# One Griffin/S5 hybrid layer on a list scheduler: landing allowance, slot choice and the order of six pieces

## The chip, the cores and the metric

One core of one Trainium2 chip. The metric is the device time of one execution in microseconds, the median of the runs. Engines are named as in the profile: PE (TensorE, matmuls), PEld (its weight loads), DVE (VectorE), ACT (ScalarE), POOL (GpSimd), SP (SyncE, which only issues transfers).

## The reference, cut to what matters

All is float32, 1024 tokens by 1024 channels, one layer:

```python
mod = silu(c) @ mod_w + mod_b                  # 9 x 1024: shift, scale, gate for three norms
u = rms_norm(x, norm1_g) * (1 + sc1) + sh1
x = x + 0.5 * g1 * ((silu(u @ Wa) * (u @ Wb)) @ ffn1_w_down)        # 2816 wide
u = rms_norm(x, norm2_g) * (1 + sc2) + sh2
xa, ga, xb, mg_a, mg_b = split(u @ w_in + b_in)
ya = rg_lru(causal_conv(xa)) * gelu(ga)                             # linear scan over the tokens
yb = gelu(s5_ssm(xb)); yb = yb * sigmoid(yb @ glu_w + glu_b)        # complex scan
m = sigmoid(mg_a) * (ya @ proj_a) + sigmoid(mg_b) * (yb @ proj_b)
x = x + g2 * (m @ w_out)
u = rms_norm(x, norm3_g) * (1 + sc3) + sh3
x = x + 0.5 * g3 * swiglu(u)                                        # ffn2
out = rms_norm(x, final_g)
```

## The kernel before

Activations lie channel-first, in tiles of 128 channels by 512 tokens (two halves h). A float32 operand is split into `hi` (rounded, on ACT) and `lo` (the rest, on DVE), and a product is three matmuls: hi·hi, hi·lo, lo·hi. Most large products are done for two output blocks at once by a seven-product scheme (`pair`): seven products of 12 matmuls each (9 or fewer in the down-projections) instead of eight. They go through four PSUM banks a, b, c, d in the order 1 (a), 6 (b), 2 (onto a), 7 (onto b), 5 (c), 4 (d), 3 (onto c). After most products ACT or DVE evicts the bank (`tmp_in<-ps_in`). `pair_weights` makes the seven weight sums: it loads b, a and a second copy of half of b, S1, into a tile `re`; POOL adds to them by accumulating transfers (`plus`, shown as `wr_in<-wr_in`), and ACT and DVE split the results into `wh` and `wl`.

Nothing is issued in the order written. Every call is recorded, and `Plan.order` lays the calls out by a list schedule: on each engine the ready call with the smallest number goes first (loads of weights count as 200 calls earlier). A call that needs a new tile starts only where its pool has a free slot. Costs come from small formulas. A transfer of 256 KB from SP is taken to land 1300 + 60 + 728 + 900 ns after its issue, and an accumulating one 1000 + 1300 + 60 + 1456 + 900 ns; the last 900 is the allowance. The free slots of a pool are a list: freed slots are appended, and `pop()` takes the last one. The engines then run their queues strictly in that order, each call waiting on semaphores for what it reads or overwrites, so a wait holds all that is queued behind it. The pools: `act` 65 slots of 512 columns, `tmp` 6, `wr` 4, `wh` and `wl` 8 each, `re` 2, `mw` 1, `ps` 8 PSUM banks.

Side work runs as generators that `spread` steps on by a rate at each `tick`: the constants of the S5 part, the columns of `mod` (a 512 KB load and a DVE product with a reduction, in tile `mw`), the S5 units and the recurrence. `finish_jobs` runs out what is left.

Stages in the trace, by time: norm 1 and the first products to 90 us, ffn1 up (with the S5 constants) to about 550, ffn1 down to 716, the mixer's input projections to 1160 (`run`: first xb, then ga and mga by pairs, then xa and mgb alternating by `IN_ORDER`), `glu` to 1185, `proj_b` to 1237, `proj_a` to 1318, `w_out` to 1410, ffn2 to the end.

Of the kernel before, what the change touches and what calls it, by code (L numbers as in the profile page):

```python
# [35 lines left out]
OUT_POOL = ((), (0, 1, 2, 3, 4, 5, 6, 7), (1, 4, 7))  # L36
LED2 = 2
S5_RATE, LRU_RATE = 0.7, 1.0
IN_ORDER = [(k, n) for n in range(8) for k in ("xa", "mgb")]

SETUP_RATE, MOD_RATE, GAIN_RATE = 1.0, 0.15, 0.1

TAGS = {
    "act": (65, 512), "tmp": (6, 512), "sd": (1, 512), "wr": (4, 1024), "wh": (8, 512), "wl": (8, 512),
# [23 lines left out]
class Plan:  # L68
# [12 lines left out]
    }  # L81
    FLEXIBLE = ("vector", "scalar", "gpsimd")

    SUM_ISSUE = 1000.0

    EXTRA = {"vector": 0.0, "scalar": 0.0, "gpsimd": 600.0}
# [162 lines left out]
    def order(self):  # L249
# [51 lines left out]
        while done < n_ops:  # L301
            for e in self.ENGINES:
                if busy[e]:
                    continue
                held, item = [], None
                while ready[e] and len(held) < 64:
                    other = heappop(ready[e])
                    n = other[1]
                    if needs[n] and not fits(n):
                        held.append(other)  # L310
                        continue
                    if item is None:
                        item = other
                        if e != "scalar" or not self.switches(n, table):
                            break
                        continue

                    if other[0] > item[0] + SAME_TABLE:
                        held.append(other)
                        break  # L320
                    if not self.switches(n, table):
                        held.append(item)
                        item = other
                        break
                    held.append(other)
                for other in held:
                    heappush(ready[e], other)
                other, late = None, []
                while e in self.FLEXIBLE and ready["either"] and len(late) < 64:
                    one = heappop(ready["either"])  # L330
                    if item is not None and item < one:
                        late.append(one)
                        break
                    if e in self.other[one[1]] and (not needs[one[1]] or fits(one[1])):
                        if soonest(one) == e:
                            other = one
                            break
                    late.append(one)
                for one in late:
                    heappush(ready["either"], one)  # L340
                if other is not None:
                    if item is not None:
                        heappush(ready[e], item)
                    item = other
                    chosen[item[1]] = e
                    engine[item[1]] = e
                if item is None:
                    continue
                n = item[1]
                for t in needs[n]:  # L350
                    g = self.tag[t]
                    self.home[t] = g, free[g].pop()
                    queue[g].pop(bisect_left(queue[g], n))
                calls = self.calls(n)
                order.append(n)
                busy[e] = True
                if calls[0][1] == "dma_start":
                    size = 1
                    for s in calls[0][2][0].shape:
                        size *= s  # L360
                    if e == "gpsimd":
                        end = now + self.SUM_ISSUE
                        dma_free = max(dma_free, end + 1300) + 60 + size * 8 / 360
                        seen = dma_free + 900
                    else:
                        dma_free = max(dma_free, now + 1300) + 60 + size * 4 / 360
                        end, seen = now + 60, dma_free + 900
                else:
                    end = now
                    for c in calls:  # L370
                        ns, t = self.cost(c, table)
                        if e == "scalar":
                            table = t
                        if self.shares_port(c):
                            end = port_free = max(end, port_free) + ns
                        else:
                            end += ns
                    until[e] = end
                    seen = end + self.LATENCY[e][1]
                heappush(events, (end, len(order), e, n, 0))  # L380
                if calls[0][1] != "dma_start":
                    heappush(events, (end + self.LATENCY[e][0], len(order), e, n, 1))
                heappush(events, (seen, len(order), None, n, 2))
# [50 lines left out]
class Layer:  # L434
# [130 lines left out]
    def pair_weights(self, srcs):  # L565

        nc = self.nc
        n = srcs[0].shape[1] // 2
        with nc.ahead(WEIGHTS_AHEAD):
            a, b = self.new("wr"), self.new("wr")  # L570
            s1 = self.new("re")[:, :n]
            nc.sync.dma_start(b[:, : 2 * n], srcs[1])
            nc.sync.dma_start(a[:, : 2 * n], srcs[0])
            nc.sync.dma_start(s1, srcs[1][:, :n])
            a1, a2, b1, b2 = a[:, :n], a[:, n : 2 * n], b[:, :n], b[:, n : 2 * n]
            nc.scalar.activation(b1, b1, AF.Copy, scale=-1.0)
            nc.plus(b1, srcs[0][:, :n])
            nc.plus(s1, srcs[1][:, n : 2 * n])
            w = {1: self.split_weight(a1)}
            nc.scalar.activation(a1, b2, AF.Copy, scale=-1.0)  # L580
            nc.plus(a1, b1)
            w[2] = self.split_weight(a2)
            nc.plus(a2, a1)
            w[6] = self.split_weight(a1)
            w[7] = self.split_weight(b1)
            w[5] = self.split_weight(s1)
            w[4] = self.split_weight(b2)
            w[3] = self.split_weight(a2)
            return {k: [v] for k, v in w.items()}
# [137 lines left out]
        nc.vector.reciprocal(r, root)  # L727
        return r

    def modulate(self, x, r, l, d, pool=False):  # L730

        nc = self.nc
        nc.vector.scalar_tensor_tensor(
            x, x, self.gsc[:, l * 8 + d : l * 8 + d + 1], r, ALU.mult, ALU.mult
        )
        hi, lo = self.act(F32R), self.act(F32R)
        nc.scalar.activation(x, x, AF.Identity, bias=self.mod(3 * l, d))
        nc.rounded(hi, x)
        nc.two(ALU.subtract, lo, x, hi.bitcast(F32))
        return hi, lo  # L740
# [496 lines left out]
class Mixer:  # L1237
# [247 lines left out]
    def run(self):  # L1485
# [7 lines left out]
        for k in range(4):  # L1493
            for i, v in enumerate(u[1][k]):
                nc.scalar.dma_start(self.u_d[2 * k + i], v.bitcast(F32))
        L.spread(self.s5_units(), S5_RATE)
        for dst, i0, fn in ((self.ga_d, 8, AF.Gelu_apprx_tanh), (self.mga_d, 20, AF.Sigmoid)):
            for i in range(i0, i0 + 8, 2):
                c11, c12, c21, c22 = L.pair(
# [12 lines left out]
        for kind, n in IN_ORDER:  # L1512
# [5 lines left out]
            for h in range(2):  # L1518
                z = L.act()
                nc.scalar.activation(z, b[h], AF.Sigmoid, bias=L.col("b_in", 28 + n))  # L1520
                nc.sync.dma_start(self.mgb_d[n][:, h * H : (h + 1) * H], z)
        L.finish_jobs()
        yb = self.glu()
        for p in range(4):
            wp = L.weight(io["proj_b"][p])
            for e in range(2):
# [4 lines left out]
                    nc.vector.tensor_mul(r, r, b[h])  # L1531
                    nc.sync.dma_start(self.q_d[d][:, h * H : (h + 1) * H], r)
        ya = [[self.load(self.ya_d, n, h) for n in range(8)] for h in range(2)]
        ya = L.pair_operands(ya[0][:4], ya[0][4:], ya[1][:4], ya[1][4:], {})
        m = [[None] * 8, [None] * 8]
        for p, pair in enumerate(PROJ_A):
            c11, c12, c21, c22 = L.pair(L.pair_weights([io["proj_a"][d] for d in pair]), ya)
# [69 lines left out]
def hybrid_layer(ctx: ExitStack, tc: tile.TileContext, io):  # L1607
# [43 lines left out]
            nc.two(ALU.subtract, lo[:, o], raw, hi.bitcast(F32)[:, o])  # L1651

    first_weights(0)
    ps = L.bank()
    for d in range(ND):
        sq = L.act()
        nc.scalar.activation(sq, x[0][d], AF.Square)
        L.mm(ps, L.ones.bitcast(F32), sq, d == 0, d == ND - 1)
    u = [[], []]

    def step(h, k):
        u[h].append(L.modulate(x[h][k], rs[h], 0, k, pool=h == 1))
        for f in range(2):
            for j in range(2):
                L.products(
# [1 line left out]
                    k == 0, k == ND - 1,  # L1667
                )

    rs = [L.rstd_of(ps)]  # L1670
    L.modulation(1, 0, "wr")
    L.modulation(0, 0, "wr")
    for d in range(ND):
        load_x(1, d)
    step(0, 0)
    L.modulation(1, 1, "wr")
    L.modulation(0, 1, "wr")
    step(0, 1)
    st = [None]
    for d in range(ND):  # L1680
        L.square(st, x[1][d], d)
    rs.append(L.rstd(st))
    first_weights(2)
    step(1, 0)
    step(1, 1)
# [17 lines left out]
            L.modulation(*c)  # L1703
            yield

    later = modulations([(i, d) for i in (2, 4, 3, 5, 7, 6) for d in range(8)])

    def background():
        L.spread(s5_setup(L), SETUP_RATE)
        L.spread(later, MOD_RATE)  # L1710

    st = [[None], [None]]
    u2 = [[], []]
# [1 line left out]
    def on_x(d, h, x):  # L1715
# [5 lines left out]
                u2[h].append(L.modulate(x[h][e], r, 1, e))  # L1721

    L.up(w_up, u, x, 2, background)
    x = L.down(
        io["ffn1_w_down"], io["x"], None, 2, on_x, [(h, slice(0, H)) for h in range(2)], PARTS[0]
    )

    t = mixer(L, u2, x, x1_d)
    pieces = [(0, slice(0, H))] + [(1, slice(i * H // LAST, (i + 1) * H // LAST)) for i in range(LAST)]
    st3 = [[None] for _ in pieces]  # L1730
# [123 lines left out]
```

## Time and profile before

| | |
|---|---|
| median of 3 runs (lowest, highest) | 2077.71 us (2075.42, 2080.06) |
| the profiled execution, its span | 2080.47 us, 2078.7 us |
| PE, DVE, ACT, POOL busy | 96%, 75%, 50%, 16% of the span |
| mean granted clock of PE | 0.985 of full |
| HBM read, written | 280.90 MB, 92.27 MB |

Busy shares are means over stages with different limits. A busy PE is not PE at its peak: the ends of matmuls are modelled. The idle time before an instruction is put down to what released it, so "PE <-ACT tmp_in" is PE waiting until ACT has read a bank out.

### The profile page before, as it was taken

How to read it: one execution, taken by the hardware profiler on the slowest of the kernel's cores; microseconds unless marked ns; L12 is line 12 of the kernel's file. 1: busy time of each engine (PE TensorE's matmuls, PEld its weight loads, DVE VectorE, ACT ScalarE, POOL GpSimd, SP SyncE). 2: the span in 40 equal slices, each digit the busy share in tenths (PEclk: the TensorE clock that was granted, in tenths of full speed). 3: DMA queues.
4: the chain of work that ended last, by engine and by line, in shares of the span. 5: the costliest groups of instructions: out<-in, count | busy, mean ns of one | idle time of the engine just before them, and what ended most of it. 6: DMA issues, size and time to landing. Idle time of an engine off the chain costs nothing. (4 is left out here: it accounts for less than half of the span.)

```text
span 2078.7 us, 27418 instructions
## 1 busy us (share of the span) xinstructions
PE 1998.8 (96%) x8852; PEld 1632.3 (79%) x8852; DVE 1565.4 (75%) x3072; ACT 1036.2 (50%) x1774; POOL 322.9 (16%) x409
## 2 busy tenths in 40 slices
PE   5999999999999999999999999999999999999997
PEld 3787777887888878778888787777888888877786
DVE  8997877789969777768886886989644444498757
ACT  5633333435433574454878942446433333366643
POOL 0122111211011011100000001100111111124442
PEclk8999999999999999999999999999999999999998
DMA  8667777889857457787544858872765666589993
GB/s 275 178 168 204 196 201 204 218 221 287 279 150 217 153 153 217 204 250 263 173 158 132 282 175 252 267 250 72 193 170 139 151 158 157 131 215 235 212 230 123
DMA packets 198704, 411.18 MB, mean 198 GB/s; under 512 B 22176, under 2 KB 48416, under 8 KB 198560
## 3 DMA queue, kind: packets, MB, share of 16 engines
q1 hardware_dynamic: 132160, 296.54, 42.7%
q0 software_dynamic: 49536, 84.96, 24.3%
q10 hardware_dynamic: 16864, 27.93, 3.6%
q8 instruction: 69, 1.13, 0.2%
q14 instruction: 75, 0.61, 0.1%
HBM read 280.90 MB, written 92.27 MB: 180 GB/s over the span
## 5 line engine op out<-in xcount | busy, mean ns | idle before, releaser
L429 PE MATMUL ps_in<-act_in,wh_in 128*128 128x512 f32 (+1 forms) x5592 | 1691.5, 391 | 47.5 <-ACT tmp_in L429 14.5
L429 PEld LDWEIGHTS ps_in<-act_in,wh_in 128*128 128x128 f32 x5592 | 1048.8, 189 | 285.4 <-ACT tmp_in L429 21.0
L429 PE MATMUL ps_in<-act_in,wl_in 128*128 128x512 f32 (+1 forms) x2796 | 1049.8, 389 | 1.0 <-DVE wl_in L429 1.0
L429 PEld LDWEIGHTS ps_in<-act_in,wl_in 128*128 128x128 f32 x2796 | 529.3, 189 | 111.1 <-DVE wl_in L429 2.1
L429 ACT ACTIVATE wh_in<-wr_in 128x512 fp32r<-128x512 f32 (+2 forms) x544 | 321.1, 599 | 524.5 <-PE ps_in L429 363.3
L429 DVE TENSOR_TENSOR wl_in<-wr_in,wh_in 128x512 fp32r<-128x512 f32 (+2 forms) x544 | 350.9, 652 | 194.2 <-ACT wh_in L429 189.7
L429 DVE TENSOR_TENSOR act_in<-act_in,act_in 128x512 fp32r<-128x512 f32 (+3 forms) x589 | 375.9, 677 | 41.1 <-ACT act_in L429 34.4
L429 DVE TENSOR_TENSOR tmp_in<-ps_in,tmp_in 128x512 f32<-128x512 f32 x296 | 203.3, 687 | 143.6 <-PE ps_in L429 133.1
L429 ACT ACTIVATE act_in<-act_in 128x512 fp32r<-128x512 f32 (+3 forms) x413 | 238.2, 614 | 144.2 <-DVE act_in L429 107.0
L429 POOL DMA_DIRECT2D wr_in<-wr_in x148 | 135.3, 914 | 556.9 <-DMA wr_in<-wr_in 205.3
L429 ACT ACTIVATE wr_in<-wr_in 128x512 f32<-128x512 f32 (+1 forms) x148 | 87.7, 598 | 86.7 <-DMA wr_in<-in_ffn_w_up 48.6
L429 ACT ACTIVATE tmp_in<-ps_in 128x512 f32<-128x512 f32 x130 | 76.2, 588 | 42.6 <-PE ps_in L429 32.6
L429 DVE TENSOR_TENSOR tmp_in<-tmp_in,ps_in 128x512 f32<-128x512 f32 x82 | 56.0, 683 | 43.4 <-PE ps_in L429 42.8
L429 ACT ACTIVATE wh_in<-re_in 128x512 fp32r<-128x512 f32 (+1 forms) x74 | 44.4, 601 | 69.3 <-PE ps_in L429 69.1
L429 DVE SCALAR_TENSOR_TENSOR mw_in<-mw_in,cact 128x1024 f32<-128x1024 f32 x56 | 68.3, 1221 | 13.8 <-DMA mw_in<-in_mod_w 13.2
L429 POOL DMA_DIRECT2D re_in<-in_ffn_w_up x40 | 34.9, 880 | 246.3 <-DVE wl_in L429 120.6
L429 DVE TENSOR_TENSOR tmp_in<-tmp_in,tmp_in 128x512 f32<-128x512 f32 (+1 forms) x96 | 65.6, 686 | 3.8 <-DMA mga_d<-tmp_in 1.9
L429 ACT ACT_TABLE_LOAD x47 | 60.3, 1283 | 12.8 <-PE ps_in L429 9.9
L429 POOL DMA_DIRECT2D wr_in<-in_ffn_w_up x40 | 35.5, 887 | 182.8 <-ACT wr_in L429 147.1
L429 PE MATMUL ps_in<-act_in,act_in 128*128 128x256 f32 (+1 forms) x336 | 56.9, 317 | 4.4 <-DMA act_in<-sty_d 1.8
L429 DVE SCALAR_TENSOR_TENSOR act_in<-ps_in,mods,act_in 128x512 f32<-128x512 f32 (+1 forms) x68 | 46.1, 684 | 19.6 <-PE ps_in L429 19.4
L429 PEld LDWEIGHTS ps_in<-act_in,act_in 128*128 128x128 f32 x336 | 48.4, 190 | 13.4 <-ACT act_in L429 2.9
(109 smaller groups left out, 997.8 us busy)
## 6 DMA issues: line engine op xcount, KB each, us to landing
wr_in<-in_ffn_w_up SPq DMA_DIRECT2D x84, 512.0 KB, 4.4
mw_in<-in_mod_w SPq DMA_DIRECT2D x56, 512.0 KB, 4.3
wr_in<-wr_in POOLq DMA_DIRECT2D x108, 256.0 KB, 4.5
g_d<-tmp_in SPq DMA_DIRECT2D x88, 256.0 KB, 4.7
act_in<-g_d SPq DMA_DIRECT2D x88, 256.0 KB, 5.8
wr_in<-in_ffn_w_down SPq DMA_DIRECT2D x48, 384.0 KB, 5.0
wr_in<-in_w_in SPq DMA_DIRECT2D x36, 512.0 KB, 4.4
x_d<-tmp_in POOLq DMA_DIRECT2D x48, 256.0 KB, 6.8
```

Of the source, the lines that this page charges most:

```text
L429: getattr(getattr(self.nc, engine), method)(*map(self.place, args), **{k: self.place(v) for k, v in kwargs.items()})
```

## The change

- `LANDING`: the allowance for a landing in the plan is 1800 ns in place of 900.
- Slots: `free[g].pop(0)` takes the slot that has been free longest, in every pool.
- `modulate`: x/rms is a DVE product of two tensors, and scale and shift are together one ACT instruction (before: DVE did x·scale/rms, ACT the shift). For the first norm a new `norm(h)` multiplies all eight tiles ahead of the first products, and the sum of squares of the second half goes through float32 matmuls with ones, as that of the first half did (before: seven DVE additions, a split, two matmuls).
- `pair_weights`: S1 is an ACT copy of the loaded half of b, not a second load.
- `IN_ORDER`: the xa blocks come earlier; `glu` stands inside the loop, after mgb 6 and before mgb 7 (before: after all).
- `proj_a`'s operands are made product by product (`pair_operands_by_product`) instead of tile by tile.
- The columns of `mod`: 24 in ffn1 up at rate 0.18 and run out there, the other 24 in the mixer at 0.2 (before: all 48 from ffn1 up on at 0.15).

```diff
+    LANDING = 1800
-                    self.home[t] = g, free[g].pop()
+                    self.home[t] = g, free[g].pop(0)
-                        seen = dma_free + 900
+                        seen = dma_free + self.LANDING
...
-                        end, seen = now + 60, dma_free + 900
+                        end, seen = now + 60, dma_free + self.LANDING
...
-            nc.sync.dma_start(s1, srcs[1][:, :n])
             a1, a2, b1, b2 = a[:, :n], a[:, n : 2 * n], b[:, :n], b[:, n : 2 * n]
+            nc.scalar.activation(s1, b1, AF.Copy)
             nc.scalar.activation(b1, b1, AF.Copy, scale=-1.0)
...
-        nc.vector.scalar_tensor_tensor(
-            x, x, self.gsc[:, l * 8 + d : l * 8 + d + 1], r, ALU.mult, ALU.mult
-        )
-        nc.scalar.activation(x, x, AF.Identity, bias=self.mod(3 * l, d))
+        if r is not None:
+            nc.two(ALU.mult, x, x, r)
+        nc.scalar.activation(
+            x, x, AF.Identity, bias=self.mod(3 * l, d),
+            scale=self.gsc[:, l * 8 + d : l * 8 + d + 1],
+        )
...
+            if n == GLU_AFTER:
+                for _ in s5:
+                    pass
+                yb = self.glu()
         L.finish_jobs()
-        yb = self.glu()
...
-        ya = L.pair_operands(ya[0][:4], ya[0][4:], ya[1][:4], ya[1][4:], {})
+        ya = L.pair_operands_by_product(ya[0][:4], ya[0][4:], ya[1][:4], ya[1][4:])
...
+    def norm(h):
+        ps = L.bank()
+        for d in range(ND):
+            sq = L.act()
+            nc.scalar.activation(sq, x[h][d], AF.Square)
+            L.mm(ps, L.ones.bitcast(F32), sq, d == 0, d == ND - 1)
+        r = L.rstd_of(ps)
+        for d in range(ND):
+            nc.two(ALU.mult, x[h][d], x[h][d], r)
```

The order on DVE, in the second pair of `proj_a`. In the rows before, wl_2614 is the lo part of a sum that POOL adds (wh_2613 is split from it); `tmp<-ps` are evictions.

```order
L429 TENSOR_TENSOR act_2594_in<-act_2594_in,ps_2587_in 128x512
L429 TENSOR_TENSOR wl_2614_in<-wr_2606_in,wh_2613_in 128x512
L429 TENSOR_TENSOR wl_2616_in<-wr_2607_in,wh_2615_in 128x512
L429 TENSOR_TENSOR act_2594_in<-act_2594_in,act_2595_in 128x512
L429 TENSOR_TENSOR tmp_2591_in<-ps_2588_in,tmp_2591_in 128x512
```

The same place now, where the sum's lo part is wl_2604.

```order
L437 TENSOR_TENSOR act_2584_in<-act_2584_in,ps_2577_in 128x512
L437 TENSOR_TENSOR wl_2606_in<-wr_2597_in,wh_2605_in 128x512
L437 TENSOR_TENSOR act_2584_in<-act_2584_in,act_2585_in 128x512
L437 TENSOR_TENSOR tmp_2581_in<-ps_2578_in,tmp_2581_in 128x512
L437 TENSOR_TENSOR wl_2604_in<-wr_2596_in,wh_2603_in 128x512
```

The eviction of the pair's second bank stood behind the split of the sum and now stands ahead of it.

The order on PE where `glu` ends; its weights are wl_2382 before and wl_2362 now, those of `proj_b` wh_2402 and wh_2393. Before:

```order
L429 MATMUL ps_2381_in<-act_2353_in,wl_2380_in 128x512
L429 MATMUL ps_2382_in<-act_2355_in,wl_2380_in 128x512
L429 MATMUL ps_2406_in<-act_2385_in,wh_2402_in 128x512
L429 MATMUL ps_2406_in<-act_2386_in,wh_2402_in 128x512
L429 MATMUL ps_2407_in<-act_2393_in,wh_2402_in 128x512
```

Now:

```order
L437 MATMUL ps_2363_in<-act_2335_in,wl_2362_in 128x512
L437 MATMUL ps_2364_in<-act_2337_in,wl_2362_in 128x512
L437 MATMUL ps_2388_in<-act_1402_in,wh_2384_in 128x512
L437 MATMUL ps_2388_in<-act_1403_in,wh_2384_in 128x512
L437 MATMUL ps_2389_in<-act_1892_in,wh_2384_in 128x512
...
L437 MATMUL ps_2388_in<-act_1416_in,wl_2387_in 128x512
L437 MATMUL ps_2389_in<-act_1460_in,wl_2387_in 128x512
L437 MATMUL ps_2397_in<-act_2367_in,wh_2393_in 128x512
```

The 48 matmuls of the last input block (mgb 7, into ps_2388 and ps_2389) now stand between the last matmul of `glu` and the first of `proj_b`; before, these two followed each other.

The order on ACT, where the weight sums of the second pair of `proj_a` are begun; `act<-act` are the operands of all pairs, `wh` the splits of the first pair. Before:

```order
L429 ACTIVATE wh_2547_in<-wr_2535_in 128x512
L429 ACTIVATE act_2509_in<-act_2502_in 128x512
L429 ACTIVATE act_2511_in<-act_2463_in 128x512
L429 ACTIVATE wr_2607_in<-wr_2607_in 128x512
L429 ACTIVATE act_2513_in<-act_2501_in 128x512
```

Now:

```order
L437 ACTIVATE act_2496_in<-act_2454_in 128x512
L437 ACTIVATE re_2598_in<-wr_2597_in 128x512
L437 ACTIVATE wh_2539_in<-wr_2524_in 128x512
L437 ACTIVATE wr_2597_in<-wr_2597_in 128x512
L437 ACTIVATE act_2498_in<-act_2455_in 128x512
```

One ACT instruction more, the copy into `re`, stands ahead of the negation of the loaded half; so it is in all 74 pairs.

## Rows read from the trace of the kernel before

**Rows 1.** The page's first part: busy us, share of span, instructions by engine.

```profile
PE 1998.8 (96%) x8852; PEld 1632.3 (79%) x8852; DVE 1565.4 (75%) x3072; ACT 1036.2 (50%) x1774; POOL 322.9 (16%) x409
```

**Rows 2.** Stretches: length, busy PE, PEld, DVE, ACT, POOL, granted clock, DMA share, GB/s.

```profile
150.00:500.00 350.00, 340.87 (x1525) 276.63 (x1525) 276.97 (x656) 139.13 (x247) 69.42 (x96) 1.00 0.77 211
...
740.00:900.00 160.00, 148.87 (x669) 121.66 (x668) 114.34 (x192) 84.92 (x135) 23.17 (x32) 0.97 0.77 213
...
1160.00:1200.00 40.00, 35.78 (x143) 28.10 (x142) 34.09 (x57) 33.57 (x56) 0.86 (x1) 0.91 0.85 299
1200.00:1310.00 110.00, 106.19 (x460) 87.07 (x460) 80.50 (x137) 41.44 (x73) 13.01 (x15) 0.98 0.77 230
1310.00:1420.00 110.00, 101.83 (x422) 81.00 (x421) 97.24 (x160) 54.78 (x91) 7.82 (x9) 0.95 0.73 227
1420.00:1830.00 410.00, 409.86 (x1809) 339.12 (x1808) 222.38 (x341) 166.65 (x287) 70.21 (x81) 1.00 0.60 149
```

**Rows 3.** What PE waited for: total us, times, longest us.

```profile
PE ps_in L429 <- ACT tmp_in L429: 20.0, 15, 3.8
...
PE ps_in L429 <- DVE tmp_in L429: 9.6, 12, 2.6
```

**Rows 4.** Timeline in ffn1 up: start, us, engine, instruction, idle before and its releaser.

```profile
297.90 1.15 ACT L429 ACTIVATE wh_in<-wr_in 128x512 fp32r<-128x512 f32 x2 [7.33 <-DMA wr_in<-wr_in]
...
299.58 0.73 PE L429 MATMUL ps_in<-act_in,wh_in 128*128 128x512 f32 x2 [0.81 <-ACT tmp_in L429]
```

**Rows 5.** Timeline in the second pair of proj_a.

```profile
1268.20 1.15 ACT L429 ACTIVATE wh_in<-wr_in 128x512 fp32r<-128x512 f32 x2 [8.08 <-DMA wr_in<-wr_in]
...
1270.68 0.68 DVE L429 TENSOR_TENSOR tmp_in<-ps_in,tmp_in 128x512 f32<-128x512 f32 x1
...
1271.42 0.72 PE L429 MATMUL ps_in<-act_in,wh_in 128*128 128x512 f32 x2 [2.63 <-DVE tmp_in L429]
```

**Rows 6.** Timeline where the mixer's first projections end.

```profile
759.89 4.32 ACTq L429 DMA_DIRECT2D u_d<-act_in  x5
...
768.55 1.22 PE L429 MATMUL ps_in<-act_in,wh_in 128*128 128x512 f32 x2 [3.82 <-ACT tmp_in L429]
```

**Rows 7.** Timeline from glu to proj_b.

```profile
1185.68 0.73 PE L429 MATMUL ps_in<-act_in,wh_in 128*128 128x512 f32 x2 [1.64 <-ACT tmp_in L429]
1187.28 0.80 PE L429 MATMUL ps_in<-act_in,wh_in 128*128 128x512 f32 x1 [0.86 <-ACT act_in L429]
1189.32 0.79 PE L429 MATMUL ps_in<-act_in,wh_in 128*128 128x512 f32 x1 [1.25 <-DVE act_in L429]
...
1187.54 9.12 DVE L429 TENSOR_TENSOR act_in<-act_in,act_in 128x256 fp32r<-128x256 f32 x16
```

**Rows 8.** Timeline in the mixer's input projections.

```profile
864.41 0.60 ACT L429 ACTIVATE tmp_in<-ps_in 128x512 f32<-128x512 f32 x1 [3.79 <-DMA ga_d<-tmp_in]
...
865.06 0.73 PE L429 MATMUL ps_in<-act_in,wh_in 128*128 128x512 f32 x2 [2.08 <-ACT tmp_in L429]
...
889.81 1.45 PE L429 MATMUL ps_in<-act_in,act_in 128*128 128x256 f32 x10 [1.77 <-DMA act_in<-sty_d]
```

**Rows 9.** Transfers: kind, count, KB each, median us from issue to landing.

```profile
wr_in<-wr_in POOLq DMA_DIRECT2D x108, 256.0 KB, 4.5
...
ga_d<-tmp_in SPq DMA_DIRECT2D x16, 256.0 KB, 5.4
```

**Rows 10.** Groups of instructions: busy us, mean ns of one, idle before.

```profile
L429 PE MATMUL ps_in<-act_in,ones 128*128 128x512 f32 x16 | 9.8, 782 | 7.7 <-DVE sd_in L429 7.7
...
L429 DVE SCALAR_TENSOR_TENSOR mw_in<-mw_in,cact 128x1024 f32<-128x1024 f32 x56 | 68.3, 1221 | 13.8 <-DMA mw_in<-in_mod_w 13.2
...
L429 ACT ACTIVATE wr_in<-wr_in 128x512 f32<-128x512 f32 (+1 forms) x148 | 87.7, 598 | 86.7 <-DMA wr_in<-in_ffn_w_up 48.6
```

**Rows 11.** Timeline at the start, the first products.

```profile
25.25 0.80 PE L429 MATMUL ps_in<-act_in,wh_in 128*128 128x512 f32 x1 [7.75 <-ACT act_in L429]
...
42.55 0.80 PE L429 MATMUL ps_in<-act_in,wh_in 128*128 128x512 f32 x1 [2.16 <-DVE act_in L429]
```

More of the change, by code (lines that the diff above doesn't have):

```diff
@@ L38 @@
 S5_RATE, LRU_RATE = 0.7, 1.0
-IN_ORDER = [(k, n) for n in range(8) for k in ("xa", "mgb")]
-SETUP_RATE, MOD_RATE, GAIN_RATE = 1.0, 0.15, 0.1
+GLU_AFTER = 6
+IN_ORDER = tuple(
+    (k, int(n)) for k, n in (v.split() for v in (
+        "xa 0", "mgb 0", "xa 1", "xa 2", "mgb 1", "xa 3", "xa 4", "mgb 2", "xa 5", "xa 6",
+        "mgb 3", "xa 7", "mgb 4", "mgb 5", "mgb 6", "mgb 7",
+    ))
+)
+SETUP_RATE, MOD_RATE, GAIN_RATE, LATE_RATE = 1.0, 0.18, 0.1, 0.2
 TAGS = {
@@ L728, in rstd_of, with modulate @@
         return r
-    def modulate(self, x, r, l, d, pool=False):
+    def modulate(self, x, r, l, d):
         nc = self.nc
-        nc.vector.scalar_tensor_tensor(
-            x, x, self.gsc[:, l * 8 + d : l * 8 + d + 1], r, ALU.mult, ALU.mult
-        )
-        hi, lo = self.act(F32R), self.act(F32R)
-        nc.scalar.activation(x, x, AF.Identity, bias=self.mod(3 * l, d))
+        if r is not None:
+            nc.two(ALU.mult, x, x, r)
+        hi, lo = self.act(F32R), self.act(F32R)
+        nc.scalar.activation(
+            x, x, AF.Identity, bias=self.mod(3 * l, d),
+            scale=self.gsc[:, l * 8 + d : l * 8 + d + 1],
+        )
         nc.rounded(hi, x)
@@ L1495, in run @@
                 nc.scalar.dma_start(self.u_d[2 * k + i], v.bitcast(F32))
-        L.spread(self.s5_units(), S5_RATE)
+        s5 = self.s5_units()
+        L.spread(s5, S5_RATE)
         for dst, i0, fn in ((self.ga_d, 8, AF.Gelu_apprx_tanh), (self.mga_d, 20, AF.Sigmoid)):
@@ L1653, in hybrid_layer @@
     first_weights(0)
[L1654 to L1658, printed above, removed]
-    u = [[], []]
+    u = [[], []]
+    def norm(h):
[7 more added lines that the diff above has]
+            nc.two(ALU.mult, x[h][d], x[h][d], r)
     def step(h, k):
-        u[h].append(L.modulate(x[h][k], rs[h], 0, k, pool=h == 1))
+        u[h].append(L.modulate(x[h][k], None, 0, k))
         for f in range(2):
@@ L1668, in step @@
                 )
-    rs = [L.rstd_of(ps)]
     L.modulation(1, 0, "wr")
     L.modulation(0, 0, "wr")
+    norm(0)
     for d in range(ND):
@@ L1678, in hybrid_layer @@
     step(0, 1)
[L1679 to L1682, printed above, removed]
+    norm(1)
     first_weights(2)
@@ L1704, in modulations @@
             yield
-    later = modulations([(i, d) for i in (2, 4, 3, 5, 7, 6) for d in range(8)])
     def background():
         L.spread(s5_setup(L), SETUP_RATE)
-        L.spread(later, MOD_RATE)
+        L.spread(modulations([(i, d) for i in (2, 4, 3) for d in range(8)]), MOD_RATE)
     st = [[None], [None]]
@@ L1723, in hybrid_layer @@
     L.up(w_up, u, x, 2, background)
+    L.finish_jobs()
     x = L.down(
@@ L1726, in hybrid_layer @@
     )
+    L.spread(modulations([(i, d) for i in (5, 7, 6) for d in range(8)]), LATE_RATE)
     t = mixer(L, u2, x, x1_d)
```

## The prediction, made before the changed kernel had run

> **What bounds the kernel now.** I read the page's busy times first. PE is busy for 96% of the span and DVE for 75% [rows 1], so a gain can only come from PE's idle time, its clock, or its work. Its work hardly changes (the rows of ones below). The windows by stage come next. From 1420 to 1830 us PE runs 1809 matmuls in 410.00 us with 0.1 us idle at clock 1.00 [rows 2], or 0.2266 us each: the well-fed pace. In the other windows a reader should see two losses, the length less PE's busy time, and length times (1 - granted clock): 9.1 and 0 us at 150 to 500, 11.1 and 4.8 at 740 to 900, 4.2 and 3.6 at 1160 to 1200, 3.8 and 2.2 at 1200 to 1310, 8.2 and 5.5 at 1310 to 1420 [rows 2]. That is 52 us; the ends of the program lose some 50 more.
>
> The waits tell whose loss it is. PE waits 20.0 us in 15 waits for ACT's reads of a bank and 9.6 us in 12 for DVE's [rows 3], the `tmp<-ps` evictions. Timelines around them show which bank PE wants. At 299.58 it waits 0.81 us while ACT stands in a split `wh<-wr` that had waited 7.33 us for an accumulated sum [rows 4]. At 1271.42 it waits 2.63 us, for an eviction that DVE did at 1270.68, behind a split held up by the 8.08 us that ACT waited for a sum [rows 5]. At 768.55 it waits 3.82 us, behind five `u_d` issues that took ACT 4.32 us [rows 6]. At 1185.68 it waits 1.64 us [rows 7]. I mapped every wait of 0.4 us or more onto the plan's slots. Thirteen of them, 16.2 us together with those four, are at the first matmul of a new tile in a bank whose last tile ended at most 13 matmuls earlier: 13 x 0.2266 = 2.9 us for an eviction that stands in line. `pop()` hands out the bank freed last, while others lie free.
>
> Some waits also cost the clock: after those at 768.55 and 1271.42 it is granted at half (1.2 of 2.4 GHz) for 6.8 and 3.4 us, and half of that, 3.4 and 1.7 us, is lost. The windows' clocks of 0.97 and 0.98 hold it [rows 2].
>
> **The change, part by part.**
>
> *Longest-free slots.* No work is added. By the new plan's slots, a new tile stands a median of 99 matmuls behind the last one into its bank (before: 14), and 12 or fewer in 2 of 513 tiles only. 99 x 0.2266 = 22 us covers each of the four waits above: the longest had ACT held for some 8 us. What goes is 16.2 + 3.4 + 1.7 = 21.3 us; I take **-20**. Bounds: -24, if smaller waits of the 29.6 us [rows 3] go too; -10, if half of the late evictions are met by the next product that accumulates onto the same bank, which the choice does not move. In the pools `wh` and `wl`, always full, the order of freeing leaves no choice: 0.
>
> *glu before the last input block.* After `glu`, PE waits 0.86 and 1.25 us at 1187.28 and 1189.32, for operands that take DVE 9.12 us [rows 7], and runs at half clock from 1187.3 to 1194.1, a loss of 3.4. Together 5.5 of the 7.8 us lost at 1160 to 1200 [rows 2]; 1.64 was counted above. Now 48 matmuls, 48 x 0.2266 = 10.9 us, lie between, against 9.12 of DVE. I take **-5**; bounds -6 and -2 (the cover is only 1.8 us longer than what it hides, and without it the waits come back ahead of `proj_b`).
>
> *Larger allowance, S1 on chip, more room in `tmp`.* The plan took a 256 KB load to land after 2.99 us and a sum after 4.72 us; now 3.89 and 5.62. The medians are 4.5 for the sums' transfers from issue to landing and 5.4 for `ga_d` [rows 9]. The second is what held ACT for 3.79 us at 864.41 and PE for 2.08 at 865.06 (with 1.7 us of half clock); 1.77 us at 889.81 wait for `sty_d` [rows 8]. Of those 5.6 us and the some 6 us at 150 to 500 that are no bank waits I take **-5**: the plan is nearer the medians, and slots used in turn leave the transfers out of `tmp` more time. Bounds 0 (the plan still does not see a landing of 8 us) and -9.
> The Trainium skill, page "DMA: Bandwidth & Descriptors", section "Anatomy of one DMA — SWDGE (gpsimd) path", has some 2.0 us fixed and the bytes at 436 GB/s on top: an estimate of 2.6 us for 256 KB on POOL's queue. By it the old allowance was ample, this term would be 0, and the sum 5 us higher. The trace disagrees: 4.5 us at the median [rows 9], and waits of 7.33 and 8.08 [rows 4, 5].
>
> *S1.* SP issues 74 loads fewer, about 19 of 411 MB. ACT makes 74 more copies at the 0.598 us of its work on `wr` [rows 10]: 74 x 0.598 = 44 us. ACT is 50% busy [rows 1] and PE need not wait for it while banks are free, so most is hidden. The copy stands ahead of the negation that the sum's transfer waits for, so each sum also starts 0.6 us later. With evictions in line behind it, bounds 0 and +7 (0.1 us a copy).
>
> *The mixer's 24 `mod` columns (before about 14 fell there).* 10 x 1.22 = 12.2 us more DVE [rows 10] and 5 MB more loads, over 400 us, of which DVE is 71% busy at 740 to 900 [rows 2]: hidden, 0. *`u_d`.* Eight issues now follow each other on ACT: 4.32 / 5 x 8 = 6.9 us [rows 6]. A bank is accumulated onto again after 12 matmuls (one product), 2.7 us, so up to 4.2 us and 3.4 of clock can show, or nothing. For these and S1 I take **+3** of 0 to +15: nearer 0, since the half clock needs a wait of PE, and the waits there lose their cause.
>
> *The head.* Eight more ones matmuls, 9.8 / 16 = 0.61 us each [rows 10], 4.9 us, run while PE stood for 7.75 us before 25.25 [rows 11]; they go on without a gap and may keep the clock at full, where 19.9 to 30.2 us is at half now. Against it the first operands wait for eight products x/rms on DVE, and the second half's first `lo` (2.16 us at 42.55 now [rows 11]) for as many. I take **-2**, bounds -5 (half of that stretch's clock loss) and +5 (the eight DVE products all in the way, at about 0.68 us each as in [rows 5]).
>
> *`modulate` and `proj_a` elsewhere.* In the second and third norms one DVE and one ACT instruction stay one each: 0. `proj_a` by product moves `lo` behind evictions at most; the order shows DVE's eviction ahead of the split, so [rows 5] cannot return in that form. The 8.2 + 5.5 us at 1310 to 1420 are waits for operands of `w_out` and for norm 3, which the change does not touch: 0. The tail: 0.
>
> Sum: -20 - 5 - 5 + 3 - 2 = **-29 us**. The profiled execution took 2080.47, so 2051.5. It lies 2.8 us above the median of the runs; in terms of the median the forecast is **2049 us**.
>
> **The rivals.**
>
> *The late evictions come back inside the pairs* (0.17). Three of seven products accumulate onto a bank that was filled 12 matmuls earlier and evicted meanwhile, and no slot choice helps them. For it: sums still land 8 us late, and ACT and DVE wait in line. Against: 13 waits are at new tiles, almost none at those products. The bank term halves to -10 and the new costs show a little: 2060, from 2055 to 2070.
>
> *The data waits go too* (0.12). If the larger allowance moves splits and loads early enough for `w_out`, the S5 units and norm 3, half of the 8.2 + 5.5 us and the rest of 150 to 500 go as well, some 16 us: 2033, from 2026 to 2038. For it: ACT's long waits for sums. Against: those operands hang on products that end just before.
>
> *Slower: S1 on ACT becomes the bound* (0.09). The copy waits for a load, and all behind it on ACT with it, evictions included. An eviction in a pair has 2.7 us less its own 0.6 before PE wants the bank; from where ACT's line leaves under 0.6 us of that, each copy reaches PE. All 74 would cost 44 us: -29 + 44 = +15, so 2093, from 2080 to 2100. For it: ACT sits behind sums and splits as it is, and in the mixer it is 53% busy at 740 to 900 [rows 2]. Against: the plan lays a copy where it thinks ACT free, and PE had no wait of this kind at the 74 negations, which wait for the same load.
>
> **How the numbers follow.** My forecast has 0.62; with the bounds, which will not all fall one way, it holds from 2035 to 2062. A measurement of this kernel can tell 0.2%, 4.2 us, from no change: 2073.6 to 2081.9. The forecast's case gives 0.58 faster, 0.03 same, 0.01 slower; the first rival 0.13, 0.03, 0.01; the second 0.12 faster; the third 0.01 same, 0.08 slower. Together faster 0.84, same 0.07, slower 0.09. The range of 2028 to 2080 leaves out nearly all of the third rival, the lower quarter of the second, and some 0.05 of the forecast's tails, 0.16 in all.
>
> **What the changed profile would show.** Slots right: PE's waits for ACT's and DVE's `tmp` fall from 29.6 us to under 12, and the clock stays 1.00 around 768 and 1272; wrong: waits of the same size at products that accumulate. glu right: no idle time and no half clock where `glu` ends. Allowance right: the waits behind `ga_d` and `sty_d` gone; wrong: new ones of 1 to 4 us elsewhere in the mixer. S1: 74 ACT copies of some 0.6 us more, SP 74 loads fewer, about 392 MB in all, no PE wait behind `re<-wr`. The head: PE without a gap from 7.7 to about 25 us. The number is wrong above all if the evictions' lateness moves rather than goes, or if loads that were in time come late under the new order.

## The result, and the profile after

| | median (lowest to highest) | ratio to before, 95% interval |
|---|---|---|
| before | 2077.71 us (2067.05 to 2090.16, 5 runs) | |
| after | 2055.88 us (2053.11 to 2057.46, 5 runs) | 0.9897 (0.9874 to 0.9920) |

The changed kernel is 21.8 us faster. The forecast was 28.7 us faster (2049 us), with a range of 2028 to 2080. The profiled execution of after took 2057.46 us, its span is 2055.7. Its busy times, against [rows 1]:

```profile
PE 1991.2 (97%) x8866; PEld 1635.7 (80%) x8866; DVE 1554.1 (76%) x3064; ACT 1065.2 (52%) x1842; POOL 324.3 (16%) x409
```

ACT has 68 instructions more: 74 copies for S1, against five table loads and one other instruction fewer. What PE waited for, with total us, times and longest us, against [rows 3]:

```profile
PE ps_in L437 <- ACT act_in L437: 15.1, 9, 5.0
PE ps_in L437 <- DVE act_in L437: 14.6, 20, 2.1
PE ps_in L437 <- ACT tmp_in L437: 10.0, 3, 3.7
...
PE ps_in L437 <- DVE tmp_in L437: 7.6, 6, 3.5
```

The waits for `tmp` fell from 29.6 to 17.6 us, not under 12 as the prediction wanted for its step. There are 9 of them in place of 27, and they are longer, 2.0 us at the mean against 1.1. Not all are evictions: at the last norm (4.0 us before, 4.1 after), and before also at the first (1.9), PE waits for an operand in `tmp` and not for a bank. The evictions proper fell from 23.7 to 13.5 us. They lie elsewhere, as PE's timeline shows (the row at 493.09 is a wait for an operand):

```profile
493.09 0.50 PE L437 MATMUL ps_in<-act_in,wh_in 128*128 128x512 f32 x1 [3.16 <-ACT act_in L437]
...
503.10 1.22 PE L437 MATMUL ps_in<-act_in,wh_in 128*128 128x512 f32 x2 [3.50 <-DVE tmp_in L437]
...
764.75 1.22 PE L437 MATMUL ps_in<-act_in,wh_in 128*128 128x512 f32 x2 [3.73 <-ACT tmp_in L437]
...
868.53 0.74 PE L437 MATMUL ps_in<-act_in,wh_in 128*128 128x512 f32 x2 [2.69 <-DVE tmp_in L437]
...
1883.28 1.22 PE L437 MATMUL ps_in<-act_in,wh_in 128*128 128x512 f32 x2 [2.65 <-ACT tmp_in L437]
```

By the plan's slots none of the four waits for an eviction is at a new tile. All are at a product that accumulates onto a bank filled 10 to 27 matmuls before. The wait behind the `u_d` issues of [rows 6] is back one product later with 3.73 us, and with its half clock (0.69 granted from 763 to 774). Of [rows 8], ACT's waits for `ga_d` and PE's for `sty_d` are gone. The 2.69 us at 868.53 have another cause: on DVE the eviction stands behind work of the S5 units.

```profile
867.18 0.69 DVE L437 TENSOR_TENSOR tmp_in<-tmp_in,tmp_in 128x510 f32<-128x510 f32 x1
867.79 0.68 DVE L437 TENSOR_TENSOR tmp_in<-ps_in,tmp_in 128x512 f32<-128x512 f32 x1
```

The windows by stage, before and then after, each with length, busy PE, PEld, DVE, ACT, POOL, granted clock, DMA share and GB/s. By the weights that PE reads, ffn1 up ends at 491 us in the kernel before, not at about 550 as the section on that kernel has it. Before: ffn1 up, ffn1 down, `proj_b`, `w_out`:

```profile
90.00:491.00 401.00, 391.43 (x1749) 318.54 (x1748) 326.81 (x913) 160.77 (x282) 80.65 (x110) 1.00 0.75 202
491.00:716.00 225.00, 224.52 (x987) 184.50 (x986) 193.40 (x342) 96.25 (x177) 24.25 (x28) 1.00 0.71 214
...
1185.00:1234.40 49.40, 46.61 (x192) 37.72 (x193) 43.88 (x76) 23.36 (x43) 3.46 (x4) 0.93 0.65 205
...
1316.60:1410.00 93.40, 86.75 (x364) 68.89 (x362) 80.64 (x134) 42.55 (x70) 6.09 (x7) 0.96 0.74 229
```

After, the same stages:

```profile
84.00:472.00 388.00, 387.56 (x1750) 321.15 (x1749) 312.06 (x875) 166.18 (x294) 80.83 (x110) 1.00 0.72 191
472.00:711.30 239.30, 230.29 (x999) 188.22 (x998) 197.86 (x359) 103.14 (x193) 22.98 (x27) 0.98 0.63 188
...
1173.50:1217.00 43.50, 43.50 (x194) 36.03 (x193) 36.93 (x64) 18.93 (x34) 5.23 (x6) 1.00 0.85 277
...
1293.50:1390.00 96.50, 86.61 (x364) 69.05 (x362) 77.17 (x125) 42.92 (x72) 6.09 (x7) 0.96 0.65 206
```

With as many matmuls, ffn1 up is 13.0 us shorter and `proj_b` 5.9. But ffn1 down is 14.3 us longer: 9.0 us of idle time in place of 0.5, and a clock of 0.98. Its 12 records more are eight small products of the S5 constants (four of them leave two records each), which the new plan runs after ffn1 up has ended. `w_out` is 3.1 longer.

To set all kernels side by side I add up over each stage what PE loses: for every matmul the time to the start of the next, less the time it takes when PE is fed (0.225 us for 512 columns, less for narrower ones). A loss counts for the stage of the next matmul, and the head holds the 7.6 us ahead of the first. Stages are told by the weights read; win+glu are the mixer's input projections and `glu`. Idle time and half clock are both in it; one profiled execution each, us:

```
            head    up1  down1  win+glu  proj_b  proj_a  w_out  ffn2  total
before      36.4   23.4    3.1     28.3     7.4     6.5   10.0  23.3  138.4
after       30.1    8.2   16.7     22.8     0.3     0.8   13.1  20.6  112.5
b_slots     35.7   22.2    7.3     25.0     8.0     6.0   11.3  22.8  138.5
b_land      35.7   14.1   12.0     18.6     8.0     0.5   17.8  24.3  131.0
b_inorder   37.9   23.6    3.1     24.8     0.6     6.9   10.9  22.7  130.5
a_rest      31.8   14.1    3.4     19.8     0.3     3.9   10.7  32.1  116.1
a_lifo      31.5   13.7   16.0     27.1     0.3     1.3   15.1  19.3  124.4
a_land900   30.5   12.1    4.7     20.9     0.3     2.8    9.6  25.1  105.9
a_s1dma     30.4    9.7   14.8     23.7     0.3     1.7   16.1  22.0  118.8
a_head      36.6    8.5   18.2     19.7     0.3     0.5   12.7  19.6  116.1
a_glu_last  30.3    8.5   18.0     24.0     0.3     0.7   14.3  18.4  114.4
a_sum1800   30.5   11.0    3.4     17.8     0.3     0.5    5.6  21.2   90.2
a900_ud     30.3   13.3    5.1     15.9     0.3     3.2    7.0  23.7   98.9
a_sum_ud    30.5   15.6    2.0     23.9     0.3     0.6    6.4  21.6  100.9
```

Kernels named b_ are the kernel before with one part of the change, those named a_ the changed kernel with something undone.

### The profile page after: what moved, and what is told of

The parts are those of the page before. It is cut to its first block, busy times and chain, and to the rows that moved or that the text cites. A ratio compares the mean times of both kernels' runs of the same rounds, so it can differ in the third digit from the quotient of the medians.

```text
span 2055.7 us, 27034 instructions
## 1 busy us (share of the span) xinstructions
PE 1991.2 (97%) x8866; PEld 1635.7 (80%) x8866; DVE 1554.1 (76%) x3064; ACT 1065.2 (52%) x1842; POOL 324.3 (16%) x409
## 5 line engine op out<-in xcount | busy, mean ns | idle before, releaser
L437 DVE TENSOR_TENSOR act_in<-act_in,act_in 128x512 f32<-128x512 f32 (+3 forms) x632 | 400.0, 677 | 30.9 <-ACT act_in L437 24.0
L437 POOL DMA_DIRECT2D x_d<-tmp_in x48 | 50.2, 1266 | 53.0 <-ACT tmp_in L437 51.5
```

Source lines behind the costliest of these rows:

```text
L437: getattr(getattr(self.nc, engine), method)(*map(self.place, args), **{k: self.place(v) for k, v in kwargs.items()})
```

## The experiments

The theory at this point: the slot choice gives about half of the gain, the moved work the rest. Rivals: the moved work alone, or the allowance, carries the change.

### Slots and allowance, alone and taken away

b_slots differs from before in one call, and a_lifo from after in the same call the other way round:

```diff
 # b_slots
-                    self.home[t] = g, free[g].pop()
+                    self.home[t] = g, free[g].pop(0)
```

> The kernel before with the longest-free slot alone. If the slot choice carries the change as forecast, its waits at new tiles (16.2 us) go and some come back at the products that accumulate: about 2066 us, 2062 to 2071, and PE's waits for evictions fall from 29.6 us to under 16. If the gain comes from the moved work and the allowance instead: within 4 us of 2077.7. Forecast term of -20 us in full: 2058.

Measured: 2076.23 us, ratio 0.9987 (0.9972 to 1.0002). By the ratio that is about 3 us, at most 6, and so the rival's case, in which the gain comes from elsewhere. PE's waits for `tmp` are 23.5 us, not under 16.

> The changed kernel with the slot freed last taken again. If the slot choice carries the change: 2064 to 2072 us (8 to 16 above 2055.9), with waits of PE at new tiles back. If with the larger allowance the evictions are in time anyway, the slot choice is worth nothing there: 2054 to 2058.

Measured: 2068.21 us, 0.9945 (0.9930 to 0.9960): 10 us above after by the ratios (4 to 16 with their intervals), as the theory had it. The same line is worth some 3 us in the one kernel and 10 in the other. What it does is the same in both: the waits of 0.4 us or more at new tiles go, from 17.0 us (the thirteen, and one in `glu`) to 0 from before to b_slots, from 7.5 to 0 from a_lifo to after. And those at products that accumulate grow, from 5.2 to 15.4 us and from 9.0 to 13.1. PE's timeline in b_slots:

```profile
498.21 1.01 PE L429 MATMUL ps_in<-act_in,wh_in 128*128 128x512 f32 x2 [2.72 <-DVE tmp_in L429]
...
845.91 0.73 PE L429 MATMUL ps_in<-act_in,wh_in 128*128 128x512 f32 x2 [2.13 <-DVE tmp_in L429]
...
1272.26 0.73 PE L429 MATMUL ps_in<-act_in,wh_in 128*128 128x512 f32 x2 [2.00 <-DVE tmp_in L429]
```

The last of these stands one product behind the place where [rows 5] had its 2.63 us: there PE accumulates onto a bank whose eviction is late too. The slot choice moved the wait and did not shorten the line in front of the evictions.

b_land differs from before by the allowance, and a_land900 from after by the same the other way round:

```diff
 # b_land
-                        seen = dma_free + 900
+                        seen = dma_free + 1800
...
-                        end, seen = now + 60, dma_free + 900
+                        end, seen = now + 60, dma_free + 1800
 # a_land900
-    LANDING = 1800
+    LANDING = 900
```

> The kernel before with the allowance of 1800 ns alone. Forecast term: -5 us, so 2073, 2068 to 2078. Rival: the allowance is what emptied ffn1 up of its losses (23.4 us before, 8.2 after the change): 2066 or less, and ACT's waits for accumulated sums (137 us in 44 waits before) clearly fewer.

Measured: 2074.01 us, 0.9968 (0.9957 to 0.9980): 6.6 us by the ratio, the forecast's case. ffn1 up is relieved as the rival had it, but other stages take that back: ffn1 up loses 9.3 us less, the mixer's projections 9.7, `proj_a` 6.0; ffn1 down loses 8.9 us more and `w_out` 7.8. ACT's waits for sums fell from 137.0 to 50.6 us.

> The changed kernel with the allowance of 900 ns. Forecast term: 5 us above 2055.9, so 2061, 2056 to 2065. Rival, the allowance carries most of the change: 2067 or more, with 10 us or more of it in ffn1 up.

Measured: 2048.35 us, 0.9855 (0.9839 to 0.9872). Both expectations have the wrong sign: without the larger allowance the changed kernel is 8.7 us faster (by the ratios; 3 to 15 with their intervals). ffn1 down loses 4.7 us in place of 16.7 and `w_out` 9.6 in place of 13.1; ffn1 up gives back 3.9. In every kernel with 1800 ns for all transfers ffn1 down loses 12 to 18 us and `w_out` 13 to 18, in every other one 2 to 7 and 6 to 11.

### The rest of the change, alone and by parts

a_rest is after with `pop()` and 900 ns.

> The changed kernel with the slot freed last and with 900 ns: norm, modulate, S1, the order of glu and the input blocks, proj_a's operands and the mod columns alone. If these carry the change (the head 6, ffn1 up 10, proj_b 7 us less lost in every kernel that has them): 2055 us, 2050 to 2061. If slots and allowance are needed beside them (rival): 2064 or more. By the forecast's terms (-5 for glu, -2 for the head, +3): 2074.

Measured: 2062.81 us, 0.9914 (0.9892 to 0.9936). The median lies between the two cases. But before had a median of 2081.57 us beside it: by the ratio the gain is 17.9 us, which from 2077.71 leads to 2059.8, in the first case. It is far from the forecast's 2074. Head, ffn1 up, the mixer's projections and `proj_b` lose 30 us less together. ffn2 loses 9 us more: with the slot freed last, waits at new tiles are back (14.2 us in the whole kernel).

With a_rest, a_lifo, a_land900 and after, slots and allowance stand in all four combinations on top of the rest of the change. Gains over before by the ratios, us:

| | 900 ns | 1800 ns |
|---|---|---|
| slot freed last | 17.9 (a_rest) | 11.4 (a_lifo) |
| slot free longest | 30.1 (a_land900) | 21.4 (after) |

There the slots are worth 10 to 12 us at either allowance, and the allowance costs 6 to 9 us at either choice; each difference is known to some 6 us. Together they add 3.5 us to the rest, which can't be told from nothing. In the kernel before, the slots were worth 3 us and the allowance 6.6.

```diff
 # a_s1dma
+            nc.sync.dma_start(s1, srcs[1][:, :n])
...
-            nc.scalar.activation(s1, b1, AF.Copy)
```

> The changed kernel with S1 loaded a second time. If the 74 loads taken from SP are what ffn1 up gained by: 2062 us, 2059 to 2067, ffn1 up losing 6 us or more again. By the forecast (S1 on ACT costs some of 3 us): 2053, 2050 to 2056.

Measured: 2062.25 us, 0.9907 (0.9883 to 0.9931). After's ratio, 0.9897, lies inside this interval (the difference is 2 us, known to some 7), so S1's place makes no difference that these runs can tell. The median stands in the first range, but ffn1 up loses 9.7 us against 8.2, so with the larger allowance it does not take the missing loads to relieve it.

```diff
 # a_head
-        r = L.rstd_of(ps)
-        for d in range(ND):
-            nc.two(ALU.mult, x[h][d], x[h][d], r)
+        rs.append(L.rstd_of(ps))
...
-        u[h].append(L.modulate(x[h][k], None, 0, k))
+        u[h].append(L.modulate(x[h][k], rs[h], 0, k))
...
-    norm(1)
+    st = [None]
+    for d in range(ND):
+        L.square(st, x[1][d], d)
+    rs.append(L.rstd(st))
```

> The changed kernel with the first norm as before: x/rms made product by product, the second half's squares added on DVE and rounded. Forecast term -2, so 2058; from the trace the head lost 6.3 us less with the change, so 2062, 2059 to 2065, with PE's half clock back between 20 and 30 us.

Measured: 2057.97 us, 0.9888 (0.9866 to 0.9911). The head loses 6.5 us more, as expected from the trace. The whole takes no longer, within some 7 us: in this profile the mixer's projections lose 3.1 and ffn2 1.0 less. What the head gains can't be told at the end.

```diff
 # a_glu_last
-            if n == GLU_AFTER:
-                for _ in s5:
-                    pass
-                yb = self.glu()
         L.finish_jobs()
+        yb = self.glu()
```

> The changed kernel with glu after the last input block, as before. Forecast term -5, so 2061; from the trace glu and proj_b lost 7.9 us less, so 2062 to 2065, with PE's idle time and half clock back at the first matmuls of proj_b. If the wait only moves: 2056.

Measured: 2054.29 us, 0.9869 (0.9844 to 0.9894): not slower, and no wait has come back there: `proj_b` loses 0.3 us. The window of `proj_b` in a_glu_last, with `glu` directly ahead of it:

```profile
1176.50:1220.00 43.50, 43.50 (x194) 36.02 (x193) 41.47 (x74) 20.41 (x37) 5.20 (x6) 1.00 0.64 188
```

PE has no idle time and full clock there without the 48 matmuls between. So the cover was not what helped. The theory that took its place rests on DVE's timeline in the kernel before, where `glu` stands from 1161 to 1185:

```profile
1175.44 1.22 DVE L429 TENSOR_TENSOR_SCAN act_in<-act_in,act_in 128x512 f32<-128x512 f32 x1
...
1177.76 1.27 DVE L429 TENSOR_TENSOR_SCAN act_in<-act_in,act_in,act_in 128x512 f32<-128x512 f32 x1
```

The scan over the tokens of the last xa block still ran on DVE there, in front of the operands. The rest of that block's recurrence ran on ACT, with table loads between the reads of `glu`'s banks:

```profile
1169.69 1.28 ACT L429 ACT_TABLE_LOAD   x1
...
1176.27 1.28 ACT L429 ACT_TABLE_LOAD   x1
```

The new `IN_ORDER` ends that block earlier; in a_glu_last the last scan starts some 14 us ahead of `glu`:

```profile
1140.50 1.28 DVE L437 TENSOR_TENSOR_SCAN act_in<-act_in,act_in,act_in 128x512 f32<-128x512 f32 x1
```

```diff
 # b_inorder
-IN_ORDER = [(k, n) for n in range(8) for k in ("xa", "mgb")]
...
+        "xa 0", "mgb 0", "xa 1", "xa 2", "mgb 1", "xa 3", "xa 4", "mgb 2", "xa 5", "xa 6",
+        "mgb 3", "xa 7", "mgb 4", "mgb 5", "mgb 6", "mgb 7",
```

> The kernel before with the new order of the input blocks alone, glu still after all of them. If proj_b waited because the scan over the tokens still ran on DVE beside glu, the earlier xa blocks alone free it: proj_b loses 1 us or less in place of 7.4, and the time is 2070, 2066 to 2073. If the 48 matmuls of the last block are what covers the operands, as forecast, proj_b still loses 6 to 8 us: 2075 to 2080.

Measured: 2071.22 us, 0.9954 (0.9941 to 0.9966), 9.6 us faster by the ratio. `proj_b` loses 0.6 us, in the window

```profile
1182.00:1225.70 43.70, 43.70 (x194) 35.78 (x193) 39.05 (x67) 21.93 (x39) 4.03 (x5) 1.00 0.58 176
```

So it is the order of the xa blocks that removes the loss, with 7.6 us at `glu` and `proj_b`. The order takes the whole recurrence of the last block out of `glu`'s way; whether the scans on DVE or the table loads on ACT held the operands was not tried apart.

### Which landing, and a faster version

```diff
 # a_sum1800: loads have 900, POOL's sums 1800
-                        end, seen = now + 60, dma_free + self.LANDING
+                        end, seen = now + 60, dma_free + 900
```

> The changed kernel with 1800 ns for POOL's accumulating transfers alone and 900 for loads. If it is the loads' allowance that puts the operands of the first down-projection and of w_out later: 2049, 2045 to 2052, those two stages losing 16 us or less together (30 with the change, 14 with 900 for all). If it is the sums': 2054 to 2058.

Measured: 2036.23 us, 0.9797 (0.9779 to 0.9815), below the range: 20 us faster than the changed kernel and 42 than before. ffn1 down and `w_out` lose 9.0 us together. ACT's waits for sums, the changed kernel, a_land900 and a_sum1800 in this order:

```profile
ACT wh_in L437 <- DMA wr_in<-wr_in: 96.1, 37, 6.9
```

```profile
ACT wh_in L437 <- DMA wr_in<-wr_in: 192.9, 57, 6.8
```

```profile
ACT wh_in L437 <- DMA wr_in<-wr_in: 34.8, 27, 4.8
```

Against a_land900 the sums' larger allowance gains 12 us by the ratios; against the changed kernel the loads' smaller one gains 21 (either to some 6 us). So it was the loads' that cost time, and the sums' that gained it. Loads stands here for all that POOL does not issue, stores included. The fourth combination, 900 for sums and 1800 for loads, was not run. The windows of ffn1 down and `w_out` in a_sum1800 have 0.5 and 4.9 us of idle time:

```profile
475.80:701.20 225.40, 224.88 (x988) 184.46 (x987) 182.01 (x309) 98.13 (x182) 22.66 (x26) 1.00 0.60 178
...
1278.00:1367.00 89.00, 84.10 (x364) 67.35 (x362) 77.51 (x123) 42.70 (x72) 6.14 (x7) 1.00 0.69 214
```

Last, the `u_d` writes:

```diff
 # a900_ud (with 900 ns), a_sum_ud (with a_sum1800)
-                nc.scalar.dma_start(self.u_d[2 * k + i], v.bitcast(F32))
+                nc.sync.dma_start(self.u_d[2 * k + i], v.bitcast(F32))
```

> The changed kernel with 900 ns and the eight u_d writes issued by SP in place of ACT. With 900 ns it took 2048.4, and PE waited 3.99 us at 757 us for an eviction behind those issues, with 3.4 us of half clock after it. If the issues on ACT are the cause: 2041, 2038 to 2044. If ACT's line is late there for other reasons: 2046 to 2050.

Measured: 2046.94 us, 0.9846 (0.9829 to 0.9863), against 0.9855 for a_land900: no difference that can be told. At the place itself it did what was expected: the wait fell from 3.99 to 1.63 us, and the clock stayed at 1.00 (755 to 766 us).

> The changed kernel with 1800 ns for sums alone and the u_d writes issued by SP. With u_d on ACT it took 2036.2, and PE waited 4.01 us at 754.78 us. With 900 ns for all, SP's issues shortened that wait from 3.99 to 1.63 us. If both gains add: 2032, 2029 to 2035. If the schedule takes the second back elsewhere: 2035 to 2040.

Measured: 2039.80 us, 0.9798 (0.9775 to 0.9820), the ratio of a_sum1800. In the profiled execution, the longest of the five (span 2043.9), ffn1 up and the mixer's projections lose 4.6 and 6.1 us more than in a_sum1800: it is another schedule, and the gain is taken back.

## Why the prediction held, and which of its steps did not

The time fell inside the range and on the forecast side, with three quarters of the forecast gain. The steps behind it did not hold as well as the sum, and that the number came out is in good part luck. The forecast had 25 of its 29 us in slots and allowance and 4 in the rest; measured, the rest alone gives 17.9 us, and slots and allowance together 3.5 on top of it.

- **Longest-free slots, -20.** Mis-sized, and the step that failed: "What goes is 16.2 + 3.4 + 1.7". (The thirteen waits add up to 16.5 in the trace.) The waits at new tiles went, to the last one. But b_slots gains 3 us (at most 6), and taking the choice from after costs 10. The first rival had the mechanism: evictions that stand in line are met inside the pairs. I gave it 0.17 because few waits of before were there: the wait at the first use had been hiding that at the second, as 1271.42 before and 1272.26 in b_slots show. The -10 that this rival left was still too much where the slots stand alone.
- **glu, -5.** Right in place and near in size (7.9 us less lost at `glu` and `proj_b`), wrong in cause. [rows 7] gave DVE's 9.12 us of operands; the 48 matmuls were read as their cover. a_glu_last has no cover and loses 0.3 us in `proj_b`, b_inorder has none and loses 0.6. What had made the operands late was the recurrence of the last xa block in front of them, on DVE and ACT, which the step did not look at. It had no term for `IN_ORDER`, which alone gives 9.6 us.
- **Larger allowance, -5.** In the kernel before, -6.6 (b_land), a hit in size. In the changed kernel it costs 8.7 us. The waits behind `ga_d` and `sty_d` went as forecast, but the step read sums and `ga_d` together [rows 9]. They part: with 1800 for the sums and 900 for loads the kernel is 20 us faster than with 1800 for both. The rows below have the medians of after, 5.1 and 5.0 us; that an allowance is nearer to the measured landing did not make the plan better for both.

```profile
wr_in<-wr_in POOLq DMA_DIRECT2D x108, 256.0 KB, 5.1
...
ga_d<-tmp_in SPq DMA_DIRECT2D x16, 256.0 KB, 5.0
```

- **S1 and new costs, +3.** Nothing that can be told (a_s1dma). The slower rival fell: the 74 copies are there, and a kernel without them is no faster. Behind `u_d` PE lost 3.73 us and the half clock, where it had lost 3.82 before: the wait is not new, but the slots' term had counted it as gone. The eight issues took ACT some 4.3 us and not 6.9: three of 0.46 us and the row below.

```profile
752.91 2.76 ACTq L437 DMA_DIRECT2D u_d<-act_in  x5
```

- **The head, -2.** The stage itself gained 6.3 us: the second half's ones matmuls without a gap, then PE waits of 2.05 and 5.00 us, in place of 7.75, 2.05 and 2.16 [rows 11]. The x16 counts records: eight such matmuls leave 16, so "eight more" are 7.13 us here and not 4.9. By a_head none of the stage's gain can be told at the end.

```profile
18.40 7.13 PE L437 MATMUL ps_in<-act_in,ones 128*128 128x512 f32 x16 [1.29 <-ACT act_in L437]
...
27.82 0.50 PE L437 MATMUL ps_in<-act_in,wh_in 128*128 128x512 f32 x1 [2.05 <-DVE act_in L437]
...
35.59 0.79 PE L437 MATMUL ps_in<-act_in,wh_in 128*128 128x512 f32 x1 [5.00 <-ACT act_in L437]
```

- **ffn1 down and `w_out`, 0.** Forecast as untouched; they lost 13.6 and 3.1 us more. With 900 ns for loads they lose 3.4 and 5.6 (a_sum1800). This is where the 7 us between forecast and result lie, and more.

So -20 was too much by 10 to 17 us, the order of the blocks and ffn1 up gave more than was counted, and the loads' allowance took some back: errors of both signs cancelled. The parts don't add either: 2.7 + 6.6 + 17.9 = 27 us alone, 21.8 together. One slip of arithmetic changes nothing: the forecast's chances add up to 0.83 faster and 0.10 slower, not 0.84 and 0.09.

Still open: what in the rest of the change relieved ffn1 up by 9 us when alone (23.4 to 14.1). In the changed kernel neither S1 nor the head makes a difference there, but the larger allowance relieves ffn1 up too; neither was taken back at 900 ns, and the mod columns' rate was not tried apart. The allowance alone does as much there (14.1), and both together more (8.2). Why the plan with the larger loads' allowance makes ffn1 down late is followed in part only. In the changed kernel at 493.09 PE waits for an operand behind a split of a sum that held ACT for 5.81 us, and at 503.10 for an eviction that DVE did behind work on the S5 constants. Their last eight small products stand inside ffn1 down in the five changed kernels with 1800 ns for loads, each with a wait of 3.5 to 4.5 us for an eviction within 15 us, and in none of the eight kernels with 900. b_land has none there and loses 12.0 us in ffn1 down all the same, so this is part of the cause at most. Which of the plan's choices put them there was not followed. ACT, then PE, then DVE:

```profile
491.99 0.52 ACT L437 ACTIVATE wh_in<-wr_in 128x384 fp32r<-128x384 f32 x1 [5.81 <-DMA wr_in<-wr_in]
```

```profile
498.15 0.63 PE L437 MATMUL ps_in<-ident,act_in 128*128 128x128 f32 x4 [0.74 <-DVE act_in L437]
```

```profile
499.53 0.69 DVE L437 TENSOR_TENSOR sd_in<-act_in,act_in 128x128 f32<-128x128 f32 x3
500.13 0.28 DVE L437 TENSOR_TENSOR act_in<-sd_in 64x128 f32<-64x128 f32 x1
500.33 0.28 DVE L437 SCALAR_TENSOR_TENSOR act_in<-sd_in 64x128 f32<-64x128 f32 x1
...
502.36 0.68 DVE L437 TENSOR_TENSOR tmp_in<-ps_in,tmp_in 128x512 f32<-128x512 f32 x1
```

## What to carry to other kernels

A wait that is seen at the first use of a resource says that something is late; moving that use away gains only what the next use does not need as early, so look at the next one before the wait is counted as gone. Where a list schedule lays out everything, price an edit by undoing it in the final kernel as well as by making it in the old one: here one line was worth 3 us or 10 to 12, and another gained 6.6 or cost 6 to 9. And split a constant that stands for two things: one allowance for sums and loads hid a gain of 20 us.

## What the runs showed of the hardware that was not expected

How long ACT waits for sums says little about the time: a_land900 has 192.9 us of it and is 8.7 us faster than the changed kernel with 96.1. PE's waits for `tmp` are 18.5 us in the one and 17.6 in the other. And the wait of PE after `u_d` came back with 3.73 to 4.01 us in after, a_land900 and a_sum1800, with the half clock behind it (0.69, 0.84 and 0.84 granted over 11 us); with the writes issued by SP it was 1.63 us in a900_ud and in a_sum_ud, and the clock stayed at 1.00. The issuing engine is not all of it: in a_rest ACT issues the writes, and the wait is 1.88 us, with 0.84 granted.
